# Merging the inverted 32-blocks of two heads in one pass in the gated DeltaNet layer

## The chip, the cores and the metric

The kernel runs on one core of one Trainium2 chip. The metric is the device time of one execution in microseconds (us). The time before is the median of three runs.

## The reference

The reference is a two-layer encoder trunk over 1040 positions (16 meta tokens and 1024 inputs, width 1024). Layer A is a gated DeltaNet with 8 heads of 128; layer B is multi-head latent attention that reads keys and values built after layer A. The change lies in layer A. Per chunk the reference solves a unit lower triangular system for u and w and then scans a state over the chunks:

```python
    decay = jnp.exp(jnp.where(tril, gc[..., :, None] - gc[..., None, :], -jnp.inf))
    kb = k * beta[..., None]
    lower = jnp.where(tril_strict, jnp.einsum('bhnid,bhnjd->bhnij', kb, k) * decay, 0.0)
    system = lower + jnp.eye(c, dtype=jnp.float32)
    rhs = jnp.concatenate([v * beta[..., None], kb * jnp.exp(gc)[..., None]], -1)
    sol = lax.linalg.triangular_solve(system, rhs, left_side=True, lower=True)
    u_base, w_dec = sol[..., :dv], sol[..., dv:]
...
    def step(state, xs):
        u0, wd, qd, att, kd, gl = xs
        u = u0 - jnp.einsum('bhck,bhkv->bhcv', wd, state)
        o = jnp.einsum('bhck,bhkv->bhcv', qd, state) + jnp.einsum('bhij,bhjv->bhiv', att, u)
        state = state * gl[..., None, None] + jnp.einsum('bhck,bhcv->bhkv', kd, u)
        return state, o
```

## The kernel before

Layer A works on 8 token tiles of 128 and the 16 meta tokens as a tile of their own, and takes chunks of 128 instead of 64, which is the same computation. The inputs to a head (key, value and query columns) each come from a GEMM in split precision (`mm3`, lines 91 to 93, three matmuls for each of eight 128-row steps, in three chunks of 272, 384 and 384 tokens), a causal convolution with SiLU (`conv_acts`: copy on ScalarE L370, first tap on GpSimd L372, three taps on VectorE L375). The weight columns are loaded on SyncE's queue (L203) and split on GpSimd or VectorE (L98, L99).

Heads are taken in pairs. For a pair, in program order: `prepare` calls `key_prep` for each head. It builds the decay matrices `att` and the strictly triangular products `U`, one 128x128 block for each token tile, and stores the 32x32 blocks on the diagonal of `U` to DRAM (`blk_in`, L462), together with the meta block `Um`. `invert_blocks` then inverts all 66 blocks of the pair at once (32 blocks and one meta block for each head, one block per partition) in 31 steps on VectorE (L525, L528), clears one triangle on GpSimd (L530) and stores the result to `blk_out` (L532).

`finish_inverse(h, N)` merges four inverted 32-blocks into one 128x128 inverse, for one head and its eight token tiles. `N` is the tile `U` itself, overwritten in place. The tile `T64` (one buffer) gets the four inverted 32-blocks of each token tile by four loads from `blk_out` (L545); VectorE transposes each into `N` (L546), 32x256 a time. The meta block takes the same way through `Xm` (one buffer, L547) and `Nm` (L548). There are then four stages, each with eight tiles of matmuls into the single bank `fin`, and an eviction of it:

1. L555, two 32x32 products a tile; VectorE multiplies by -beta into `T64` (L557, twice).
2. L560 and L562, three 32x32 products a tile; ScalarE copies them to `T64` and `N` (L563, and L565 twice).
3. L568, one 64x64 product a tile; VectorE multiplies by -beta (L569).
4. L572, one 64x64 product a tile; ScalarE copies to `N` (L573).

A float32 matmul is two instructions in the trace. The result `N` is read by the scan (`scan_tile`, L600), and `Nm` by `scan_meta` (L579). The scans of the two heads alternate by token tile and share the bank tag `ch`; a scan step goes from PE to VectorE and back several times (L595, L597, L599, L600, L602, L605, L607, L609).

The program is written in the order of the main loop (below), but each engine's order of issue is set when the kernel is built: instructions whose inputs are expected to be ready can be issued ahead of earlier ones that are expected to wait, by program order otherwise. So GEMM matmuls of the next heads stand between the stages of the merge and the steps of the scan on PE, and parts of the next pair's `key_prep` start before the scan has ended. Each engine then runs its own queue strictly in that order; semaphores make an instruction wait, and all behind it on that engine.

Of the kernel before, what the change touches and what calls it, by code (L numbers as in the profile page):

```python
# [16 lines left out]
F32 = mybir.dt.float32  # L17
# [3 lines left out]
ALU = mybir.AluOpType  # L21
PSUM = bass.MemoryType.PSUM

P = 128
D = 1024
NM = 16
T = 1024
L = NM + T
NT = T // P
# [87 lines left out]
def body(ctx: ExitStack, tc: tile.TileContext, I, out):  # L117
    nc = tc.nc
    V, A, G, TE, SY = nc.vector, nc.scalar, nc.gpsimd, nc.tensor, nc.sync
    tpool, nm, act, mm3, split_w, split_ps = tools(tc)  # L120
# [11 lines left out]
    blk_out = [dram(f"blk_out{i}", [66, 32, 32]) for i in range(2)]  # L132
# [49 lines left out]
    with ExitStack() as la:  # L182
# [5 lines left out]
        def bank(tag, shape):  # L188
            return pp.tile(shape, F32, tag=tag, name=nm(tag), bufs={'mm': 2, 'tr': 3, 'fin': 1, 'ch': 2}[tag])
# [25 lines left out]
        with ExitStack() as l0:  # L215
# [9 lines left out]
            n = 0  # L225
# [15 lines left out]
            for c, (a, b) in enumerate(TOKC):  # L241
                tiles = [t for t in range(-1, NT) if a <= tok(t)[0] < b]
# [12 lines left out]
                for kt in range(KT):  # L255
                    ps = bank("tr", [P, 512])
# [4 lines left out]
        with ExitStack() as l0:  # L261
# [8 lines left out]
            for c, (a, b) in enumerate(TOKC):  # L270
                ps = bank("fin", [P, 512])[0:4 * H, 0:b - a]
                for kt in range(KT):
                    w = wab2[:, kt].rearrange("p x c -> p (x c)")
# [5 lines left out]
            ps = bank("tr", [P, 512])  # L279
            for t in range(-1, NT):  # L280
                a, b = tok(t)
# [13 lines left out]
            def ntile(name, w=NT + 1):  # L295
# [4 lines left out]
            beta, g, egc, ekd, necb, egl, epsq, nbeta = (ntile(x) for x in (  # L300
                "beta", "g", "egc", "ekd", "necb", "egl", "epsq", "nbeta"))
# [20 lines left out]
            ps = bank("tr", [P, 512])  # L322
# [17 lines left out]
        kp = ld.enter_context(tpool(name="kA", bufs=2))  # L340
        sp = ld.enter_context(tpool(name="sA", bufs=2))
        bp = ld.enter_context(tpool(name="bA", bufs=1))
# [37 lines left out]
        def halves():  # L380
            return [(hf, slice(4 * hf, 4 * hf + 4)) for hf in range(2)]

        def key_prep(h, kn):

            att, kd = ([kp.tile([P, 4, P], F32, tag=y, name=nm(y), bufs=6) for _ in range(2)] for y in ("att", "kd"))
            U = kp.tile([P, NT, P], F32, tag="U", name=nm("U"), bufs=4)
            kdm = sp.tile([NM, P], F32, tag="kdm", name=nm("kdm"), bufs=3)
            hc = slice(h, h + 1)
            flat = lambda x: x.rearrange("p a b -> p (a b)")
# [2 lines left out]
            for half, s4 in halves() + [(2, slice(NT, NT + 1))]:  # L392
                k, tiles = (P, range(s4.start, s4.stop)) if half < 2 else (NM, (-1,))
                ps = bank("tr", [P, 4, P])
                junk = sp.tile([P, P], BF16, tag="jk", name=nm("junk"), bufs=1)
                for j, t in enumerate(tiles):
                    a, b = tok(t)
# [5 lines left out]
                if half < 2:  # L403
                    V.tensor_tensor(out=kd[half], in0=ps, in1=sc4[:, :, None].broadcast_to([P, 4, P]),
                                    op=ALU.mult)
                else:
                    V.tensor_scalar(out=kdm, in0=ps[0:k, 0, :], scalar1=sc4, scalar2=None, op0=ALU.mult)
            for rows, s in ((slice(0, P), slice(0, NT)), (slice(0, NM), slice(NT, NT + 1))):
                x = lambda y: flat(y[rows, s, hc])
# [4 lines left out]
            ps = bank("tr", [P, 512])  # L414
# [9 lines left out]
            for half, s4 in halves():  # L424
                ps = bank("tr", [P, 512])
                for i in range(2):
                    s2 = slice(s4.start + 2 * i, s4.start + 2 * i + 2)
                    gs = [bp.tile([P, 2, P], F32R, tag=f"g{y}", name=nm("gm")) for y in range(2)]
                    for y, gy in enumerate((ghi, glo)):
# [5 lines left out]
                                op=ALU.mult)  # L435
                G.affine_select(out=att[half], in_=att[half], compare_op=ALU.is_ge, fill=0.0, base=0,
                                pattern=[[0, 4], [1, P]], channel_multiplier=-1)
                ps = bank("tr", [P, 512])
                for j in range(4):
                    a, b = tok(4 * half + j)  # L440
                    TE.matmul(ps[:, P * j:P * j + P], kn[:, a:b], kn[:, a:b], start=True, stop=True)
                V.tensor_tensor(out=U[:, s4, :], in0=ps.rearrange("p (t i) -> p t i", i=P),
                                in1=att[half], op=ALU.mult)
            attm = sp.tile([NM, NM], F32, tag="attm", name=nm("attm"), bufs=3)
# [4 lines left out]
            ps = bank("tr", [P, 512])  # L449
# [11 lines left out]
                r = slice(32 * q, 32 * q + 32)  # L461
                SY.dma_start(dst[q], U[r, :, r])  # L462
            SY.dma_start(blk_in[gi][33 * hl + 32, 0:NM, 0:NM], Um)
            return dict(att=att, attm=attm, U=U, kd=kd, kdm=kdm)

        def query_prep(h, c):

            qT, kn, att, attm = c["qT"], c["kn"], c["att"], c["attm"]
            sq = kp.tile([P, L], F32, tag="vT", name=nm("sq"), bufs=1)
            ps = bank("tr", [P, 512])  # L470
            for a, b in TOKC:
                act(sq[:, a:b], qT[:, a:b], AF.Square)
            for t in range(-1, NT):
                a, b = tok(t)
                s = t if t >= 0 else NT
                TE.matmul(ps[0:b - a, s:s + 1], sq[:, a:b], one, start=True, stop=True)
            for rows, s in ((slice(0, P), slice(0, NT)), (slice(0, NM), slice(NT, NT + 1))):
                V.tensor_scalar(out=epsq[rows, s, h:h + 1].rearrange("p t o -> p (t o)"), in0=ps[rows, s],
                                scalar1=EPS * P, scalar2=EPS * EPS * P, op0=ALU.mult, op1=ALU.add)
            for half, s4 in halves():  # L480
                ps = bank("tr", [P, 512])
                for j in range(4):
                    a, b = tok(4 * half + j)
                    TE.matmul(ps[:, P * j:P * j + P], kn[:, a:b], qT[:, a:b], start=True, stop=True)  # L484
                V.tensor_tensor(out=att[half], in0=ps.rearrange("p (t i) -> p t i", i=P),
                                in1=att[half], op=ALU.mult)
            ps = bank("tr", [P, 512])
            TE.matmul(ps[:NM, 0:NM], kn[:, 0:NM], qT[:, 0:NM], start=True, stop=True)
            V.tensor_tensor(out=attm, in0=ps[:NM, 0:NM], in1=attm, op=ALU.mult)
# [41 lines left out]
                            channel_multiplier=0)  # L531
            SY.dma_start(blk_out[gi].rearrange("p a b -> p (a b)"), flat)  # L532

        def finish_inverse(h, N):

            gi, hl = (h // 2) % 2, h % 2
            Nm = sp.tile([32, 32], F32, tag="Nm", name=nm("Nm"), bufs=3)
            Xm = bp.tile([32, 32], F32, tag="Xm", name=nm("Xm"))
            T64 = bp.tile([P, NT, 64], F32, tag="T64", name=nm("T64"))
            q0, q1, q2, q3 = qs = [slice(32 * q, 32 * q + 32) for q in range(4)]  # L540
            lo32, hi32 = slice(0, 32), slice(32, 64)
            G.memset(T64[q0, :, hi32], 0.0)
            blk = blk_out[gi][33 * hl:33 * hl + 32].rearrange("(t q) i j -> q i t j", q=4)
            for q, c in ((0, lo32), (1, hi32), (2, lo32), (3, hi32)):
                SY.dma_start(T64[qs[q], :, c], blk[q])  # L545
                V.transpose(N[qs[q], :, qs[q]], T64[qs[q], :, c])  # L546
            SY.dma_start(Xm, blk_out[gi][33 * hl + 32])  # L547
            V.transpose(Nm, Xm)  # L548
            bt = lambda rows, w: nbeta[rows, 0:NT, h:h + 1].broadcast_to([rows.stop - rows.start, NT, w])
            ps = bank("fin", [P, NT, 64])  # L550
            Z = T64[:, :, lo32]
            lo64, hi64 = slice(0, 64), slice(64, P)
            for t in range(NT):
                for a, b in ((q0, q1), (q2, q3)):
                    TE.matmul(ps[b, t, 0:32], N[a, t, b], T64[a, t, 0:32], start=True, stop=True)  # L555
            for b in (q1, q3):
                V.tensor_tensor(out=Z[b], in0=ps[b, :, 0:32], in1=bt(b, 32), op=ALU.mult)  # L557
            ps = bank("fin", [P, NT, 64])
            for t in range(NT):
                TE.matmul(ps[q1, t, 0:32], N[q1, t, q1], Z[q1, t, :], start=True, stop=True)  # L560
                for a, b in ((q0, q1), (q2, q3)):
                    TE.matmul(ps[a, t, 32:64], Z[b, t, :], N[b, t, b], start=True, stop=True)  # L562
            A.copy(T64[q1, :, 0:32], ps[q1, :, 0:32])  # L563
            for a, b in ((q0, q1), (q2, q3)):
                A.copy(N[a, :, b], ps[a, :, 32:64])  # L565
            ps = bank("fin", [P, NT, 64])
            for t in range(NT):
                TE.matmul(ps[hi64, t, :], N[lo64, t, hi64], T64[lo64, t, :], start=True, stop=True)  # L568
            V.tensor_tensor(out=T64[hi64], in0=ps[hi64], in1=bt(hi64, 64), op=ALU.mult)  # L569
            ps = bank("fin", [P, NT, 64])  # L570
            for t in range(NT):
                TE.matmul(ps[lo64, t, :], T64[hi64, t, :], N[hi64, t, hi64], start=True, stop=True)  # L572
            A.copy(N[lo64, :, hi64], ps[lo64])  # L573
            return dict(N=N, Nm=Nm[0:NM, 0:NM])

        def scan_meta(h, c):
            ps = bank("ch", [P, 512])
# [42 lines left out]
        def keys_of(h):  # L620
            hs[h]["kn"] = conv_acts(D + h * P, "kn", 4)
# [8 lines left out]
            hs[h]["vb"], hs[h]["vbm"] = natural(hs[h]["vT"], beta, h, "vb")  # L630

        def prepare(h0):
            for h in (h0, h0 + 1):
                hs[h].update(key_prep(h, hs[h]["kn"]))
            invert_blocks((h0 // 2) % 2, h0)

        def finish(h):
            hs[h].update(finish_inverse(h, hs[h]["U"]))

        keys_of(0)  # L640
        keys_of(1)
# [1 line left out]
        for h0 in range(0, H, 2):  # L643
            h1, more = h0 + 1, h0 + 2 < H
            values_of(h0)
            value_rows(h0)
            values_of(h1)
            queries_of(h0)
            value_rows(h1)
            queries_of(h1)  # L650
            query_prep(h0, hs[h0])
            finish(h0)
            if more:
                keys_of(h0 + 2)
            query_prep(h1, hs[h1])
            if more:
                keys_of(h1 + 2)
            finish(h1)
            Ss = {h: scan_meta(h, hs[h]) for h in (h0, h1)}
            for t in range(NT):  # L660
                for h in (h0, h1):
                    Ss[h] = scan_tile(h, t, hs[h], Ss[h])
            if more:
                prepare(h0 + 2)
# [791 lines left out]
```

## Time and profile before

| | |
|---|---|
| median of 3 runs | 1362.63 us |
| lowest, highest | 1353.95 us, 1364.2 us |
| the profiled execution | 1358.79 us, span 1357.1 us |
| granted TensorE clock in it, mean | 0.989 |
| busy: PE, VectorE, ScalarE, GpSimd | 1313.5, 905.6, 537.2, 408.7 us |

The profile is of one execution. PE is TensorE's matmuls, PEld its weight loads, DVE VectorE, ACT ScalarE, POOL GpSimd, SP (SPq) SyncE, which issues the DMAs. L555 is line 555 of the kernel. In a group of instructions `fin<-T,U` names what is written and what is read (`T` is `T64`, buffer numbers are left out); then come the shapes, the count after an x, and the least, median and longest duration in ns. In the order of time the columns are start and duration in us, and in brackets the idle time ahead of the instruction and what ended it; a row with x16 stands for sixteen instructions in a row, from the start of the first to the end of the last. In the list of waits the columns are the total in us, how many, and the longest. Layer A takes the first half of the span, up to about 640 us.

### The profile page before, as it was taken

How to read it: one execution, taken by the hardware profiler on the slowest of the kernel's cores; microseconds unless marked ns; L12 is line 12 of the kernel's file. 1: busy time of each engine (PE TensorE's matmuls, PEld its weight loads, DVE VectorE, ACT ScalarE, POOL GpSimd, SP SyncE). 2: the span in 40 equal slices, each digit the busy share in tenths (PEclk: the TensorE clock that was granted, in tenths of full speed). 3: DMA queues.
4: the chain of work that ended last, by engine and by line, in shares of the span. 5: the costliest groups of instructions: out<-in, count | busy, mean ns of one | idle time of the engine just before them, and what ended most of it. 6: DMA issues, size and time to landing. Idle time of an engine off the chain costs nothing.

```text
span 1357.1 us, 24958 instructions
## 1 busy us (share of the span) xinstructions
PE 1313.5 (97%) x9064; PEld 1184.5 (87%) x9064; DVE 905.6 (67%) x2625; ACT 537.2 (40%) x1706; POOL 408.7 (30%) x684
## 2 busy tenths in 40 slices
PE   6999999999999999999999999998999999999998
PEld 4879989988998999898788798887999999998887
DVE  6679768968996895545464665323887879778321
ACT  6442243233324331211132243115777777776200
POOL 3344223423342130042010401321544445337100
PEclk9999989999999999999999999999999999999999
DMA  6111112121111213126552202312111101014443
GB/s 186 39 27 46 46 24 52 48 49 31 50 47 36 47 47 91 54 82 206 173 167 87 83 13 64 109 66 69 36 42 32 54 24 41 17 36 136 136 149 111
DMA packets 116924, 96.81 MB, mean 71 GB/s; under 512 B 28462, under 2 KB 106094, under 8 KB 116802
## 3 DMA queue, kind: packets, MB, share of 16 engines
q1 hardware_dynamic: 116802, 95.23, 23.3%
q8 instruction: 71, 1.16, 0.4%
q14 instruction: 51, 0.42, 0.1%
HBM read 68.19 MB, written 27.01 MB: 70 GB/s over the span
## 4 chain that ended last, share of the span: by engine, by line
PE 76%; DVE 8%; POOL 6%; ACT 4%; DMA 3%; issue 2%; SPq 0%; DVEq 0%; POOLq 0%; ACTq 0%
PE mm L93 7%; PE mm L91 7%; PE mm L92 7%; PE sc L93 6%; PE sc L92 6%; PE sc L91 6%; PE bd L91 4%; PE bd L92 4%; PE bd L93 4%; PE pt L1298 2%; PE tr L484 1%; PE ch L599 1%; PE ch L595 1%; ACT junk L82 1%; PE ch L609 1%
## 5 line engine op out<-in xcount | busy, mean ns | idle before, releaser
L91 PE MATMUL mm<-hT_hi,whi 128*128 128x384 f32 (+1 forms) x768 | 257.0, 335 | 2.4 <-DVE whi L98 2.4
L93 PE MATMUL mm<-hT_hi,wlo 128*128 128x384 f32 (+1 forms) x768 | 256.0, 333 | 0.5 <-DVE wlo L99 0.5
L92 PE MATMUL mm<-hT_lo,whi 128*128 128x384 f32 (+1 forms) x768 | 255.4, 333 | 0.0
L91 PEld LDWEIGHTS mm<-hT_hi,whi 128*128 128x128 f32 x768 | 146.8, 191 | 4.0 <-issue 2.9
L93 PEld LDWEIGHTS mm<-hT_hi,wlo 128*128 128x128 f32 x768 | 146.9, 191 | 3.3 <-DVE wlo L99 1.1
L92 PEld LDWEIGHTS mm<-hT_lo,whi 128*128 128x128 f32 x768 | 147.2, 192 | 1.3 <-issue 0.8
L108 DVE TENSOR_TENSOR pTl<-pt,pTh 128x256 fp32r<-128x256 f32 (+2 forms) x112 | 55.0, 494 | 11.0 <-ACT pTh L107 9.6
L98 POOL TENSOR_SCALAR whi<-raw 128x512 fp32r<-128x512 f32 x48 | 38.5, 816 | 73.2 <-PE mm L92 67.1
L82 ACT ACTIVATE P<-P,mx 128x144 f32<-128x144 f32 (+3 forms) x64 | 50.6, 791 | 21.3 <-DVE mx L1256 18.7
L91 PE MATMUL sc<-wo_hi,oTh 128*128 128x512 f32 (+1 forms) x144 | 57.6, 400 | 0.6 <-issue 0.6
L93 PE MATMUL sc<-wo_hi,oTl 128*128 128x512 f32 (+1 forms) x144 | 57.2, 397 | 0.0
L92 PE MATMUL sc<-wo_lo,oTh 128*128 128x512 f32 (+1 forms) x144 | 57.0, 396 | 0.0
L370 ACT COPY z<-mm 128x384 f32<-128x384 f32 (+1 forms) x72 | 31.8, 442 | 62.1 <-PE mm L93 61.6
L99 DVE TENSOR_TENSOR wlo<-raw,whi 128x512 fp32r<-128x512 f32 x64 | 47.3, 745 | 10.6 <-POOL whi L98 10.4
L375 DVE SCALAR_TENSOR_TENSOR kn<-z,pcol,kn 128x384 f32<-128x384 f32 (+1 forms) x72 | 42.3, 589 | 17.4 <-POOL kn L372 16.5
L107 ACT CAST pTh<-pt 128x256 fp32r<-128x256 f32 (+2 forms) x112 | 47.2, 427 | 14.6 <-PE pt L1298 7.2
L1269 POOL TENSOR_SCALAR P<-P,sl 128x144 f32<-128x144 f32 (+3 forms) x64 | 51.5, 806 | 3.7
L1267 POOL TENSOR_SCALAR Pe<-P,sl 128x128 f32<-128x128 f32 x64 | 29.5, 462 | 73.3 <-DVE sl L1264 55.6
L93 PE MATMUL sc<-h_hi,wlo 128*128 128x512 f32 x128 | 50.8, 397 | 0.0
L92 PE MATMUL sc<-h_lo,whi 128*128 128x512 f32 x128 | 50.6, 396 | 0.0
L91 PE MATMUL sc<-h_hi,whi 128*128 128x512 f32 x128 | 50.5, 395 | 0.0
L102 DVE SCALAR_TENSOR_TENSOR wlo<-raw,pcol,whi 128x128 fp32r<-128x128 f32 x64 | 23.4, 429 | 40.3 <-POOL whi L101 40.3
(380 smaller groups left out, 3985.4 us busy)
## 6 DMA issues: line engine op xcount, KB each, us to landing
raw<-in_a_w_in SPq DMA_DIRECT2D x64, 256.0 KB
xt<-in_x SPq DMA_DIRECT2D x16, 512.0 KB
o_scr<-o SPq DMA_DIRECT2D x64, 64.0 KB
raw<-in_a_w_out SPq DMA_DIRECT2D x8, 512.0 KB
on<-o_scr SPq DMA_DIRECT2D x8, 512.0 KB
x_scr<-xt SPq DMA_DIRECT2D x8, 512.0 KB
raw<-in_b_w_in SPq DMA_DIRECT2D x8, 512.0 KB
gb_scr<-z SPq DMA_DIRECT2D x8, 512.0 KB
```

The source lines that it names most:

```text
L82: i = A.activation(out_ap, in_ap, func, **kw)
L91: TE.matmul(ps, ahi, bhi, start=first, stop=False)
L92: TE.matmul(ps, ahi, blo, start=False, stop=False)
L93: TE.matmul(ps, alo, bhi, start=False, stop=last)
L98: eng.tensor_scalar(out=hi, in0=raw, scalar1=1.0, scalar2=1.0, op0=ALU.mult, op1=ALU.mult)
L99: V.tensor_tensor(out=lo, in0=raw, in1=hi, op=ALU.subtract)
L107: A.copy(hi, ps)
L108: V.tensor_tensor(out=lo, in0=ps, in1=hi, op=ALU.subtract)
L370: A.copy(z[:, 3 + a:3 + b], gemm_T(hi, lo, c))
L375: V.scalar_tensor_tensor(out=yc, in0=z[:, a + j:b + j], scalar=col("cw", 24 * j + m), in1=yc, op0=ALU.mult, op1=ALU.add)
L1267: G.tensor_scalar(out=Pe, in0=Pm[:, None, 0:NM].broadcast_to([P, E8, NM]), scalar1=s, scalar2=1.0, op0=ALU.mult, op1=ALU.mult)
L1269: G.tensor_scalar(out=Pm[:, 0:n], in0=Pm[:, 0:n], scalar1=s, scalar2=1.0, op0=ALU.mult, op1=ALU.mult)
```

## The change

The two heads of a pair are merged in one pass. `U` becomes one tile `[P, 2, NT, P]` for a pair (2 buffers instead of 4 of half the size), and `T64` becomes `[P, 2, NT, 64]` (still one buffer). `finish_inverses(h0, N)` does what `finish_inverse` did for both heads: it loads the eight block groups first (quadrants in the order 0, 2, 1, 3, both heads of each), then takes the two meta blocks through `Xm` and `Nm`, then transposes each quadrant for both heads by one instruction of 32x512. Stages 1 and 2 put each head's products beside the other's in the bank `fin`, packed to 32 columns. In stages 3 and 4 the heads use different halves of the partitions of the bank (`to`): in stage 3 head 0 the upper half and head 1 the lower, in stage 4 the other way round. Evictions of stages 1 and 2 are done for both heads by one instruction, those of stages 3 and 4 head by head. In each stage the tiles of head 1 come first, then those of head 0.

In the main loop the one call stands behind the first of the next pair's keys and ahead of the second head's query preparation; before, the first head's call stood ahead of those keys, and the second head's behind the second of the next pair's keys, directly ahead of the scan.

```diff
-        def finish_inverse(h, N):
+        def finish_inverses(h0, N):
...
-            T64 = bp.tile([P, NT, 64], F32, tag="T64", name=nm("T64"))
+            T64 = bp.tile([P, 2, NT, 64], F32, tag="T64", name=nm("T64"))
...
-            G.memset(T64[q0, :, hi32], 0.0)
-            blk = blk_out[gi][33 * hl:33 * hl + 32].rearrange("(t q) i j -> q i t j", q=4)
-            for q, c in ((0, lo32), (1, hi32), (2, lo32), (3, hi32)):
-                SY.dma_start(T64[qs[q], :, c], blk[q])
-                V.transpose(N[qs[q], :, qs[q]], T64[qs[q], :, c])
-            SY.dma_start(Xm, blk_out[gi][33 * hl + 32])
-            V.transpose(Nm, Xm)
+            G.memset(T64[q0, :, :, hi32], 0.0)
+            cs = (lo32, hi32, lo32, hi32)
+            for q in (0, 2, 1, 3):
+                for hl in range(2):
+                    blk = blk_out[gi][33 * hl:33 * hl + 32].rearrange("(t q) i j -> q i t j", q=4)
+                    SY.dma_start(T64[qs[q], hl, :, cs[q]], blk[q])
+            for hl in range(2):
+                Nm = sp.tile([32, 32], F32, tag="Nm", name=nm("Nm"), bufs=3)
+                Xm = bp.tile([32, 32], F32, tag="Xm", name=nm("Xm"))
+                SY.dma_start(Xm, blk_out[gi][33 * hl + 32])
+                V.transpose(Nm, Xm)
+                Nms.append(Nm[0:NM, 0:NM])
+            tiles = lambda x: x.rearrange("p h t i -> p (h t) i")
+            for q, c in enumerate(cs):
+                V.transpose(tiles(N[qs[q], :, :, qs[q]]), tiles(T64[qs[q], :, :, c]))
...
+            each = [(hl, t) for hl in (1, 0) for t in range(NT)]
+            Z = T64[:, :, :, lo32]
+            ps = bank("fin", [P, 2, NT, 32])
+            for hl, t in each:
+                for a, b in ((q2, q3), (q0, q1)):
+                    TE.matmul(ps[b, hl, t], N[a, hl, t, b], T64[a, hl, t, 0:32], start=True, stop=True)
+            for b in (q1, q3):
+                V.tensor_tensor(out=Z[b], in0=ps[b], in1=bt(b, 0, 2, 32), op=ALU.mult)
+            ps = bank("fin", [P, 2, NT, 32])
+            for hl, t in each:
+                TE.matmul(ps[q1, hl, t], N[q1, hl, t, q1], Z[q1, hl, t], start=True, stop=True)
+                for a, b in ((q0, q1), (q2, q3)):
+                    TE.matmul(ps[a, hl, t], Z[b, hl, t], N[b, hl, t, b], start=True, stop=True)
+            A.copy(T64[q1, :, :, 0:32], ps[q1])
+            for a, b in ((q0, q1), (q2, q3)):
+                A.copy(N[a, :, :, b], ps[a])
+
             ps = bank("fin", [P, NT, 64])
+            to = ((hi64, lo64), (lo64, hi64))
+            for hl, t in each:
+                TE.matmul(ps[to[hl][0], t], N[lo64, hl, t, hi64], T64[lo64, hl, t], start=True, stop=True)
+            for hl in range(2):
+                V.tensor_tensor(out=T64[hi64, hl], in0=ps[to[hl][0]], in1=bt(hi64, hl, 1, 64)[:, 0], op=ALU.mult)
             ps = bank("fin", [P, NT, 64])
+            for hl, t in each:
+                TE.matmul(ps[to[hl][1], t], T64[hi64, hl, t], N[hi64, hl, t, hi64], start=True, stop=True)
+            for hl in range(2):
+                A.copy(N[lo64, hl, :, hi64], ps[to[hl][1]])
+            for hl in range(2):
+                hs[h0 + hl].update(N=N[:, hl], Nm=Nms[hl])
...
         def prepare(h0):
+            U = kp.tile([P, 2, NT, P], F32, tag="U", name=nm("U"), bufs=2)
             for h in (h0, h0 + 1):
-                hs[h].update(key_prep(h, hs[h]["kn"]))
+                hs[h].update(key_prep(h, hs[h]["kn"], U[:, h - h0]))
...
             query_prep(h0, hs[h0])
-            finish(h0)
             if more:
                 keys_of(h0 + 2)
+            finish_inverses(h0, hs[h0]["Us"])
             query_prep(h1, hs[h1])
             if more:
                 keys_of(h1 + 2)
-            finish(h1)
             Ss = {h: scan_meta(h, hs[h]) for h in (h0, h1)}
```

More of the change, by code (lines that the diff above doesn't have):

```diff
@@ L381, in halves, with key_prep @@
             return [(hf, slice(4 * hf, 4 * hf + 4)) for hf in range(2)]
-        def key_prep(h, kn):
+        def key_prep(h, kn, U):
             att, kd = ([kp.tile([P, 4, P], F32, tag=y, name=nm(y), bufs=6) for _ in range(2)] for y in ("att", "kd"))
-            U = kp.tile([P, NT, P], F32, tag="U", name=nm("U"), bufs=4)
             kdm = sp.tile([NM, P], F32, tag="kdm", name=nm("kdm"), bufs=3)
@@ L463, in key_prep @@
             SY.dma_start(blk_in[gi][33 * hl + 32, 0:NM, 0:NM], Um)
-            return dict(att=att, attm=attm, U=U, kd=kd, kdm=kdm)
+            return dict(att=att, attm=attm, kd=kd, kdm=kdm)
         def query_prep(h, c):
@@ L532, in invert_blocks @@
             SY.dma_start(blk_out[gi].rearrange("p a b -> p (a b)"), flat)
-        def finish_inverse(h, N):
-            gi, hl = (h // 2) % 2, h % 2
-            Nm = sp.tile([32, 32], F32, tag="Nm", name=nm("Nm"), bufs=3)
-            Xm = bp.tile([32, 32], F32, tag="Xm", name=nm("Xm"))
-            T64 = bp.tile([P, NT, 64], F32, tag="T64", name=nm("T64"))
+        def finish_inverses(h0, N):
+            gi = (h0 // 2) % 2
+            Nms = []
+            T64 = bp.tile([P, 2, NT, 64], F32, tag="T64", name=nm("T64"))
@@ L548, in finish_inverse @@
-            V.transpose(Nm, Xm)
-            bt = lambda rows, w: nbeta[rows, 0:NT, h:h + 1].broadcast_to([rows.stop - rows.start, NT, w])
-            ps = bank("fin", [P, NT, 64])
[L551 to L557, printed above, removed]
@@ L558, in finish_inverse @@
-            ps = bank("fin", [P, NT, 64])
[L559 to L574, printed above, removed]
+            G.memset(T64[q0, :, :, hi32], 0.0)
@@ new lines, in finish_inverses, with bt @@
+            tiles = lambda x: x.rearrange("p h t i -> p (h t) i")
+            for q, c in enumerate(cs):
+                V.transpose(tiles(N[qs[q], :, :, qs[q]]), tiles(T64[qs[q], :, :, c]))
+            def bt(rows, hl, n, w):
+                y = nbeta[rows, 0:NT, h0 + hl:h0 + hl + n].rearrange("p t h -> p h t")
+                return y[:, :, :, None].broadcast_to([rows.stop - rows.start, n, NT, w])
+            each = [(hl, t) for hl in (1, 0) for t in range(NT)]
+            Z = T64[:, :, :, lo32]
@@ new lines, in finish_inverses @@
+            lo64, hi64 = slice(0, 64), slice(64, P)
+            ps = bank("fin", [P, 2, NT, 32])
[9 more added lines that the diff above has]
+                    TE.matmul(ps[a, hl, t], Z[b, hl, t], N[b, hl, t, b], start=True, stop=True)
@@ L632, in prepare @@
         def prepare(h0):
+            U = kp.tile([P, 2, NT, P], F32, tag="U", name=nm("U"), bufs=2)
             for h in (h0, h0 + 1):
-                hs[h].update(key_prep(h, hs[h]["kn"]))
+                hs[h].update(key_prep(h, hs[h]["kn"], U[:, h - h0]))
+            hs[h0]["Us"] = U
             invert_blocks((h0 // 2) % 2, h0)
-        def finish(h):
-            hs[h].update(finish_inverse(h, hs[h]["U"]))
         keys_of(0)
```

## The prediction

> **What bounds the kernel now.** I read the page first, for the engine that sets the end and the one profiled execution's span.
>
> ```profile
> span 1357.1 us, 24958 instructions
> PE 1313.5 (97%) x9064; PEld 1184.5 (87%) x9064; DVE 905.6 (67%) x2625; ACT 537.2 (40%) x1706; POOL 408.7 (30%) x684
> PE   6999999999999999999999999998999999999998
> PE 76%; DVE 8%; POOL 6%; ACT 4%; DMA 3%; issue 2%; SPq 0%; DVEq 0%; POOLq 0%; ACTq 0%
> ```
>
> TensorE (PE) is busy 97% of the span, nine tenths or more in all but three of the forty slices, and makes up 76% of the chain that ended last. So the change is worth what it saves or costs in PE's own queue. The next view is the busy time by stretch, where I put the bounds round the places at which the inverse is merged and the scan runs (161 to 210 us for the first pair of heads, then 290 to 335, 415 to 460, 540 to 590), with one stretch of plain GEMM work (460 to 540) to compare.
>
> ```profile
> core 0: us, PE busy (x) PEld busy (x) DVE busy (x) ACT busy (x) POOL busy (x), PEclk, DMA share, GB/s
> 161.00:210.00 49.00, 47.47 (x467) 40.40 (x466) 35.48 (x123) 21.25 (x89) 12.62 (x26) 0.90 0.12 27
> 290.00:335.00 45.00, 44.05 (x472) 37.95 (x473) 34.46 (x119) 20.04 (x88) 11.96 (x23) 1.00 0.15 36
> 415.00:460.00 45.00, 44.57 (x472) 37.49 (x471) 35.16 (x127) 19.63 (x82) 10.41 (x23) 1.00 0.13 30
> 460.00:540.00 80.00, 79.70 (x614) 76.05 (x613) 63.42 (x177) 21.20 (x59) 14.95 (x18) 1.00 0.25 68
> 540.00:590.00 50.00, 50.00 (x443) 44.78 (x441) 29.51 (x94) 12.11 (x47) 1.95 (x2) 1.00 0.19 59
> ```
>
> Even where the merges and the scan run, PE is idle for only 1.53 + 0.95 + 0.43 + 0.00 = 2.91 us in all: the projection GEMMs of the next heads fill the waits. VectorE (DVE) has 10 to 20 us free in each of these four stretches. A shorter chain of merges is therefore worth little in itself; what counts is how much PE time the merges use.
>
> **The change part by part: PE.** The query on the tile of the merge bank (fin) gives every instruction of the merges.
>
> ```profile
> L555 PE MATMUL fin<-T,U x256: 190/191/258, 161.9 to 548.9; 32*32 32x32 f32 x128
> L562 PE MATMUL fin<-U,T x256: 190/191/213, 166.7 to 551.2; 32*32 32x32 f32 x128
> L560 PE MATMUL fin<-T,U x128: 185/191/213, 166.7 to 551.1; 32*32 32x32 f32 x128
> L568 PE MATMUL fin<-T,U x128: 218/218/268, 171.3 to 553.5; 64*64 64x64 f32 x128
> L572 PE MATMUL fin<-U,T x128: 217/218/366, 174.5 to 555.7; 64*64 64x64 f32 x128
> L557 DVE TENSOR_TENSOR T<-fin,nbeta x16: 417/424/431, 165.2 to 550.0; 32x256 f32<-32x256 f32 x16
> L565 ACT COPY U<-fin x16: 361/362/365, 169.5 to 552.1; 32x256 f32<-32x256 f32 x16
> L569 DVE TENSOR_TENSOR T<-fin,nbeta x8: 694/694/695, 172.5 to 553.8; 64x512 f32<-64x512 f32 x8
> L573 ACT COPY U<-fin x8: 578/579/582, 176.5 to 555.9; 64x512 f32<-64x512 f32 x8
> ```
>
> The matmuls stay: the new loops run over two heads and eight tiles, so the five rows keep 256, 256, 128, 128 and 128 instructions, with the same 32 by 32 and 64 by 64 shapes. What goes is visits. Between two stages of a head PE does other work, and each time it goes to the small shapes and comes back. Order of time on PE shows what that costs:
>
> ```profile
> 311.73 0.33 PE L92 MATMUL mm<-hT_lo,whi 128*128 128x384 f32 x1
> 311.90 0.34 PE L93 MATMUL mm<-hT_hi,wlo 128*128 128x384 f32 x1
> 312.16 1.14 PE L572 MATMUL fin<-U,T 64*64 64x64 f32 x16
> 313.24 0.28 PE L417 MATMUL tr<-ident,br 128*8 128x128 f32 x1
> ...
> 184.22 0.69 PE L555 MATMUL fin<-T,U 32*32 32x32 f32 x30
> 184.84 0.17 PE L418 MATMUL tr<-ident,br 16*1 16x16 f32 x1
> ```
>
> One GEMM matmul follows the last by 0.17 us (311.73 to 311.90), but the first L572 follows by 0.26: 0.09 us to get in. Sixteen L572 take 1.14 us to the end of the last, which itself lasts 0.218: fifteen steps of 0.92 / 15 = 0.061. From the first to the next foreign instruction are 1.08 us, so the last step is 1.08 - 0.92 = 0.16, or 0.10 to get out. For L555, thirty in 0.69 with 0.191 for the last make steps of 0.017; 0.62 to the next instruction leaves 0.12, again 0.10 to get out. A visit costs 0.09 + 0.10 = 0.19 us beside its matmuls.
>
> [...]
>
> How many visits? Four stages a head, and the first comes in two pieces, as the chain shows:
>
> ```profile
> 181.87 0.24 PE fin L555 x2
> 184.29 0.62 PE fin L555 x30
> ```
>
> So 5 visits for each of 8 heads, 40 in all; with a pair in one pass, 5 for each of 4 pairs, 20. **20 x 0.19 = 3.8 us saved.** The bounds: nothing, if the order of issue cuts the longer stages up again, and 20 x 0.26 = 5.2 if the first matmul's whole step of 0.26 went.
>
> **DVE and ScalarE (ACT).** From 32x256 to 64x512 a DVE eviction grows from 424 to 694 ns, 1.05 ns a column and about 154 ns for the instruction; an ACT copy grows from 362 to 579, about 145 ns for the instruction. A pair loses 2 multiplies and 3 copies: 0.31 us of DVE and 0.43 of ACT. The block transposes fall from 8 to 4; no 32x512 transpose is in the trace, so a merged one lies between one and two of the present ones:
>
> ```profile
> L546 DVE STREAM_TRANSPOSE U<-T x32: 425/435/442, 162.4 to 549.5; 32x256 f32<-32x256 f32 x32
> ```
>
> 0.44 to 0.87 us; I take 0.71, by the slope of the evictions, which saves 4 x 0.16 = 0.6 us a pair. All of it lies beside PE work, since DVE has 10 us and more free in each stretch: 0 in the sum, at most the 4 x 0.9 = 3.6 us of DVE if the GEMMs that cover it were gone.
>
> **GpSimd (POOL).** The memset of T64 waits for the tile's one buffer, until the head before has ended its last stage, and POOL's queue stands behind it:
>
> ```profile
> POOL T L542 <- PE fin L572: 30.2, 4, 16.3
> ...
> 176.57 0.30 POOL L542 MEMSET T<- 32x256 f32 x1 [8.25 <-PE fin L572]
> 180.99 0.41 POOL L430 TENSOR_SCALAR_AFFINE_SELECT gm<-ghi 128x256 fp32r<-128x256 f32 x1 [4.12 <-PE tr L432]
> ```
>
> With one tile for both heads this wait goes. But what is late next is PE: POOL's next instruction after the memset waits 4.12 us for a PE matmul, so POOL was not what PE missed. I take 0, with -1 us as the far end (a third of the 2.91 idle).
>
> **SyncE and the meta block.** Ten loads a pair stay ten, but the eight block loads now stand ahead of both Xm loads, and the two Xm transposes ahead of all block transposes. Xm has one buffer, so the second load waits for the first transpose:
>
> ```profile
> 159.17 1.82 SPq L545 DMA_DIRECT2D T<-blk_out  x4
> 161.03 0.45 SPq L547 DMA_DIRECT2D Xm<-blk_out  x1
> 166.77 0.31 SPq L547 DMA_DIRECT2D Xm<-blk_out  x1
> 170.38 0.20 DVE L548 STREAM_TRANSPOSE Nm<-Xm 32x32 f32<-32x32 f32 x1 [0.49 <-DMA Xm<-blk_out]
> ...
> PE ch L579 <- DVE Nm L548: 1.6, 2, 1.3
> ```
>
> An Xm load took 170.38 - 166.77 = 3.6 us from issue to use. That turn exists now, and PE waits 1.6 us in all for it at the meta scan (L579). In the new order the block transposes can stand behind two such turns in DVE's queue; behind those stand the conv steps of the next keys (L375), for which ACT and then the next key preparation wait. Stage 1 needs no transpose, so PE can start it; stage 2 is what would be late. Costs between -1.6 (the L579 wait goes) and 4 x 7.2 = 28.8 (both turns bare in four pairs); I take 0, nearest to the row of 1.6 in all, because GEMMs are ready for PE there. Weight loads queue behind the second Xm load on SyncE as they do now. [...]
>
> **Order.** Moving the pass behind the next pair's first keys costs nothing, as the block loads can't start before the inversion ends: in the first pair they are issued at 159.17, and L555 begins 2.7 us later, at 161.9. The second head's merge comes earlier, before its query preparation; its scan can begin with the other's. PE has the same work to do, so 0 in the sum, at most the 2.91 us of idle.
>
> **Sum.** -3.8 us. The profiled execution took 1358.79 us (span 1357.1 and 1.7 around it), so one like it would take 1355.0. The median of the three runs shown, 1362.63, lies 3.8 us higher; on that footing the forecast is 1358.8.
>
> **The rivals.**
> - *Cut up again.* The change doesn't do what it says: other work is issued between the halves of the merged stages, as between the 2 and the 30 of L555. Visits stay near 40, time 1362.6. For: that cut exists in the chain now; against: the 16 and 30 matmul runs above are otherwise unbroken.
> - *Everything falls into place.* The 3.8 us, the 2.91 us of idle and the 1 to 2 us of slower steps around them go: -8, 1354.6. To pass 1% it would need 13.6 us, which no row shows in these stretches.
> - *The Xm turns are bare* (slower). DVE stands at the second Xm transpose, the block transposes wait, PE reaches stage 2 with its order fixed and waits. With one turn bare in each pair 4 x 3.6 - 3.8 = +10.6, 1373.2; with both 4 x 7.2 - 3.8 = +25.0, 1387.6. It passes 1% from (13.6 + 3.8) / 4 = 4.4 us of bare wait a pair. For: PE does wait for Nm at L579. Against: DVE has stood for a block load before, 6.25 us up to 531.51, and PE was idle 0.30 us in the whole stretch from 460 to 540:
>
> ```profile
> 531.51 1.42 DVE L546 STREAM_TRANSPOSE U<-T 32x256 f32<-32x256 f32 x3 [6.25 <-DMA T<-blk_out]
> ```
>
> **How the numbers follow.** Forecast 0.56, cut up again 0.18, everything in place 0.13, bare turns 0.13. A change of 1% (13.6 us) is about what a measurement of this kernel can tell from none: the runs shown lie between 1353.95 and 1364.2. Faster by over 1%: half of the good case and a little for an order that I don't see, 0.10. Slower by over 1%: half of the bare turns and as much for order, 0.10. Within 1%: 0.80. The range goes from 1349 (the good case, and half the 10.2 us spread of the runs shown below it) to 1375 (one turn bare in each pair, and 2 us of spread): it leaves out about 0.10 on each side.
>
> **What would show it.** Right: the five matmul rows keep their counts, and runs of 32 and about 60 stand in PE's order of time where 16 and 30 stood; the multiplies of stage 1 are 8 of 32x512 at about 0.69 us, the copies 12 at about 0.58, the transposes 16; POOL's wait of 30.2 us is gone and the span hardly shorter for it; PE idle in the four stretches stays under 3 us. Wrong: a long wait of DVE for Xm ahead of the block transposes with PE idle at stage 2, runs still of 16 and 30, steps inside a run other than 0.061 and 0.017, or a change of many us in stretches without merges, which would mean that the order of all the rest has moved.

## The result and the profile after

The changed kernel takes 1351.3 us in the median of 14 runs (1347.6 to 1355.0), the kernel before, on the same chip, 1361.5. The ratio is 0.9938 (95% interval 0.9921 to 0.9955), or 8.4 us less. A second comparison, of 12 runs, gave 1352.1 and a ratio of 0.9950 (0.9925 to 0.9975). The forecast was 1358.8, 3.8 us less than the 1362.6 of the three runs before: right in sign and inside its range, with under half of the gain. Both profiled executions ran at the same mean clock, 0.989, so the pages can be set side by side. First the page of the changed kernel:

```profile
span 1350.1 us, 24895 instructions
PE 1306.3 (97%) x9064; PEld 1181.7 (88%) x9064; DVE 900.1 (67%) x2601; ACT 534.8 (40%) x1694; POOL 412.8 (31%) x680
```

The span is 7.0 us shorter and PE's busy time 7.2. PE executes 9064 matmuls as before, so nearly all of the gain is that the same matmuls take less of PE's time; a drop in PE's idle time is not where it lies. The busy time by stretch, with the bounds of before:

```profile
161.00:210.00 49.00, 48.50 (x524) 42.76 (x523) 40.14 (x141) 23.82 (x94) 14.79 (x31) 1.00 0.13 31
290.00:335.00 45.00, 44.49 (x358) 40.03 (x357) 37.67 (x136) 18.46 (x77) 14.56 (x30) 1.00 0.11 24
415.00:460.00 45.00, 44.69 (x360) 41.16 (x358) 36.01 (x126) 17.27 (x69) 11.69 (x25) 1.00 0.14 32
460.00:540.00 80.00, 79.15 (x697) 75.23 (x696) 56.91 (x149) 18.71 (x49) 18.42 (x14) 0.98 0.24 64
540.00:590.00 50.00, 50.00 (x343) 47.21 (x342) 26.59 (x83) 10.00 (x40) 15.16 (x10) 1.00 0.27 80
```

PE's idle in the four stretches falls from 2.91 to 1.32 us, but rises from 0.30 to 0.85 between 460 and 540, into which the last pair's merges (up to 535) now fall. The granted clock, the number behind POOL's, is 1.00 in the first stretch, where it was 0.90.

The merge bank's instructions, by tile, and the order of time on PE in the first pair:

```profile
L566 PE MATMUL fin<-T,U x256: 190/191/212, 163.5 to 522.2; 32*32 32x32 f32 x128
L573 PE MATMUL fin<-U,T x256: 191/191/212, 167.6 to 527.2; 32*32 32x32 f32 x128
L571 PE MATMUL fin<-T,U x128: 191/191/212, 167.5 to 527.2; 32*32 32x32 f32 x128
L581 PE MATMUL fin<-T,U x128: 218/218/267, 172.2 to 530.9; 64*64 64x64 f32 x128
L586 PE MATMUL fin<-U,T x128: 218/218/267, 176.5 to 535.3; 64*64 64x64 f32 x128
L568 DVE TENSOR_TENSOR T<-fin,nbeta x8: 683/690/698, 165.4 to 523.2; 32x512 f32<-32x512 f32 x8
L576 ACT COPY U<-fin x8: 574/576/577, 170.3 to 528.6; 32x512 f32<-32x512 f32 x8
L574 ACT COPY T<-fin x4: 576/577/577, 169.7 to 527.5; 32x512 f32<-32x512 f32 x4
```

```profile
163.46 1.20 PE L566 MATMUL fin<-T,U 32*32 32x32 f32 x64
164.59 0.33 PE L397 MATMUL tr<-ident,kn 128*128 128x128 f32 x1
...
172.15 1.90 PE L581 MATMUL fin<-T,U 64*64 64x64 f32 x32
173.98 0.71 PE L597 MATMUL ch<-um,kdm 16*128 16x128 f32 x4
```

All five counts and durations are kept. Stage 1 is one run of 64, stages 3 and 4 are runs of 32. Only stage 2 is cut: 4 of its 96 instructions come 0.9 us ahead of the rest here, up to 1.9 us in the other pairs. By the records there are 20 visits where there were 40; counted as runs with nothing between, 23 and 42, since in three of the new runs and two of the old a single 16x16 matmul of the meta scan (L595; L579 in the kernel before) stands in the middle.

### The profile page after: what moved, and what is told of

The parts are those of the page before. It is cut to its first block, busy times and chain, and to the rows that moved or that the text cites. A ratio compares the mean times of both kernels' runs of the same rounds, so it can differ in the third digit from the quotient of the medians.

```text
span 1350.1 us, 24895 instructions
## 1 busy us (share of the span) xinstructions
PE 1306.3 (97%) x9064; PEld 1181.7 (88%) x9064; DVE 900.1 (67%) x2601; ACT 534.8 (40%) x1694; POOL 412.8 (31%) x680
## 4 chain that ended last, share of the span: by engine, by line
PE 75%; DVE 8%; DMA 5%; POOL 5%; ACT 4%; issue 3%; SPq 0%; DVEq 0%; ACTq 0%; POOLq 0%
PE mm L91 7%; PE mm L93 7%; PE mm L92 7%; PE sc L93 6%; PE sc L92 6%; PE sc L91 6%; PE bd L91 3%; PE bd L93 3%; PE bd L92 3%; PE pt L1312 2%; PE tr L483 1%; DMA raw<-in_a_w_out 1%; ACT junk L82 1%; DMA out<-raw 1%; PE ch L625 1%
## 5 line engine op out<-in xcount | busy, mean ns | idle before, releaser
L91 PE MATMUL bd<-wf_hi,oTh 128*128 128x512 f32 x128 | 50.2, 392 | 0.3 <-ACT oTh L1422 0.2
```

The source lines that it names most:

```text
L91: TE.matmul(ps, ahi, bhi, start=first, stop=False)
```

## The experiments

One more column of the results is needed to read them. Executions of one kernel differ by several us, and each time goes with its mean granted clock: fitted over the runs of each kernel with 12 or 14 runs, 0.001 of clock stands for 0.7 to 1.4 us. (As an estimate from the span: if half clock for D us loses D/2 of work, 0.001 of mean clock is 1.36 us where PE's clock sets the pace.)

| kernel | median us | ratio to before (95%) | mean clock |
|---|---|---|---|
| before | 1359.1 to 1361.5 | 1 | 0.987 |
| changed | 1351.3; 1352.1 | 0.9938; 0.9950 (intervals above) | 0.989 |
| x1: new place alone | 1360.0 | 1.0002 (0.9971 to 1.0032) | 0.987 |
| y1: changed, all stages head by head | 1359.9 | 1.0005 (0.9987 to 1.0023) | 0.982 |
| x2: changed, stages 3 and 4 head by head | 1365.5 | 1.0039 (1.0011 to 1.0068) | 0.978 |
| y4: before, two buffers for T64 | 1361.0 | 0.9994 (0.9962 to 1.0026) | 0.985 |
| y2: before, two buffers for Xm | 1358.1 | 0.9998 (0.9977 to 1.0019) | 0.986 |
| x4: before, both | 1361.8 | 0.9998 (0.9969 to 1.0026) | 0.983 |
| x3: changed, 64 small matmuls added | 1383.4 | 1.0177 (1.0137 to 1.0216) | 0.979 |
| x6: x2 with dense matmuls added | 1360.2 | 0.9999 (0.9979 to 1.0019) | 0.991 |
| x7: changed, norms spread out | 1356.1 | 0.9954 (0.9935 to 0.9973) | 0.990 |
| x5: changed, heads take turns | 1347.5 | 0.9894 (0.9871 to 0.9918) | 0.989 |
| y3: x5, two buffers for Xm | 1347.9 | 0.9914 (0.9889 to 0.9939) | 0.987 |

The changed kernel ran again beside the first of them:

> The changed kernel once more, to stand beside the others on one chip. Theory A (visits: PE pays about 0.2 us each time it goes to the small shapes and back, and 20 such visits go) gives -4 us of the 8 to 10 us measured and leaves the rest open. Theory B (order: the second head's merge and scan start earlier, whatever the number of visits) gives all 8 to 10. Both expect about 8 us below before here.

**The place alone (x1).** The kernel before, with both calls at the new place:

```diff
             query_prep(h0, hs[h0])
-            finish(h0)
             if more:
                 keys_of(h0 + 2)
+            finish(h0)
+            finish(h1)
             query_prep(h1, hs[h1])
...
-            finish(h1)
             Ss = {h: scan_meta(h, hs[h]) for h in (h0, h1)}
```

> The kernel before, its two separate merges called one after the other at the place of the changed kernel's one call; 40 visits stay. Theory A: within 2 us of before (no visit goes). Theory B: 8 us faster than before, like the changed kernel. If both have a part: about 4 us faster.

1360.0, ratio 1.0002: the place alone gives nothing, within the 4 us of the interval. The pass at the old place was not run.

**Sharing alone (y1, x2).** y1 keeps the place, the paired loads, the paired transposes and the pair's `T64`, and does the matmul stages head by head, each with its own bank. x2 does so for stages 3 and 4 only:

```diff
-            for hl, t in each:
-                TE.matmul(ps[to[hl][0], t], N[lo64, hl, t, hi64], T64[lo64, hl, t], start=True, stop=True)
+            for hl in (0, 1):
+                ps = bank("fin", [P, NT, 64])
+                for t in range(NT):
+                    TE.matmul(ps[hi64, t], N[lo64, hl, t, hi64], T64[lo64, hl, t], start=True, stop=True)
...
```

> The changed kernel with all four matmul stages of the merges done head by head again, each with its own bank: 40 visits to the small modes where the changed kernel has 20 to 23, while the paired block loads, the paired transposes, the pair's 64-tile (so no wait of POOL for it) and the place in the program stay. Theory of the visits (0.24 us each, counted in the trace of before): 17 to 20 visits more, 4 to 5 us slower than the changed kernel at the same granted clock, so 1356 to 1357 at 0.989; where the longer stretch of small matmuls also lowers the clock, as stages 3 and 4 alone by head did (0.978), 1362 to 1366. Theory of the waits (what the changed kernel gained at equal clock is the 30.2 us of POOL's waiting and the single buffers): equal to the changed kernel at the same clock, 1351 to 1352 at 0.989.

> The changed kernel with stages 3 and 4 head by head again (two more evictions of the bank in a row, 28 visits instead of 20). Theory A: 8 visits more, 8 x 0.2 = 1.6 us slower than the changed kernel, so about 6.5 us faster than before. Theory B: as the changed kernel. If the longer chain through the one bank counts: 4 us or more slower than the changed kernel.

y1 measured 1359.9: in the measured time all of the gain is gone, so sharing the stages is worth about 8 us, and the loads, the transposes and the single memset show nothing without it. But the theory of the visits alone gave 1356 to 1357, and the clock is lower too, 0.982 for 0.989. Runs at one clock, 0.985 to 0.986, divide it otherwise: 15 of the kernel before took 1362.3 us in the mean, three of y1 1355.9, two of the changed kernel 1353.9. They are few, but by them y1 keeps most of the gain at an equal clock, sharing is worth some 2 us there, and the rest of its 8 us is the clock. x2 is slower still at 0.978. Its trace, by stretch, shows the clock at one half in the merges' last stages, with PE busy all the time:

```profile
170.00:176.30 6.30, 5.87 (x54) 4.53 (x55) 4.57 (x20) 2.14 (x6) 0.76 (x2) 1.00 0.01 3
176.30:186.60 10.30, 10.30 (x61) 9.21 (x59) 3.30 (x8) 2.61 (x9) 1.94 (x5) 0.50 0.01 2
```

The kernel before has such a stretch too, and the changed one has none there (PE alone, before first, then changed):

```profile
172.80:183.00 10.20, 10.20 (x49) 0.50 0.09 14
```

```profile
172.80:183.00 10.20, 10.20 (x109) 1.00 0.01 2
```

In these 10.20 us the kernel before issues 49 matmuls and the changed one 109. They aren't the same matmuls, but the next lines of before show the price for one and the same group, stage 4 at half clock and at full (the first is from the first head's merge):

```profile
174.49 1.97 PE L572 MATMUL fin<-U,T 64*64 64x64 f32 x16
...
191.85 1.14 PE L572 MATMUL fin<-U,T 64*64 64x64 f32 x16
192.92 0.49 PE L599 MATMUL ch<-S,qT 128*128 128x128 f32 x2
193.25 0.39 PE L600 MATMUL ch<-r,U 128*128 128x128 f32 x2
193.47 0.38 PE L398 MATMUL tr<-ident,kn 128*128 128x128 f32 x2
```

To divide the gain I went through all PE steps between 100 and 600 us of four traces: each step from one start to the next, less the median step of that instruction outside half-clock stretches.

```
us between 100 and 600               before  changed    y1     y4
lost at half clock                     12.0      8.7   13.5   18.6
visits (in, out, the step after)       10.2      4.6    8.8    8.4
time inside the runs of merges         24.5     22.4   24.3   24.2
other steps late by over 0.1           14.5     15.8   14.9   10.1
```

From before to changed: -5.6 for the visits, -2.1 inside the runs, -3.3 at half clock, +1.3 for other late steps. Over the whole span the half-clock losses are equal (16.3 and 16.2 us), so the two profiles' 7.0 us are, by this count, the visits and the runs (7.7, less the 1.3). In the medians another 2 us or so are clock (0.987 to 0.989). For y1 the count divides the 8 us less sharply: visits and runs 6.1, half clock 7.9 over the span, which is 3.6 more than the 10.4 us between the two spans; and y1's clock alone, at 0.7 to 1.36 us for 0.001, makes 5 to 9. How much of sharing's 8 us is visits and how much clock stays open: 6.1 us of visits and runs by this count of y1's one profiled execution (1362.2 us, the third slowest of its twelve), some 2 us by the runs at one clock.

**The waits (y4, y2, x4).** Two buffers in the kernel before, for `T64`, for `Xm`, for both:

```diff
-            Xm = bp.tile([32, 32], F32, tag="Xm", name=nm("Xm"))
-            T64 = bp.tile([P, NT, 64], F32, tag="T64", name=nm("T64"))
+            Xm = bp.tile([32, 32], F32, tag="Xm", name=nm("Xm"), bufs=2)
+            T64 = bp.tile([P, NT, 64], F32, tag="T64", name=nm("T64"), bufs=2)
```

> The kernel before with two buffers instead of one for T64 and for Xm; nothing merged, 40 visits stay. The waits of GpSimd for T64 (30.2 us in the profile before) and of the second Xm load go. Theory A (visits and the clock): within 2 us of before. Theory C (the waits for the single buffers are what the merge took away): 6 to 8 us faster.

> The kernel before with two buffers for the 64-tile alone: POOL's wait of 30.2 us in all is gone and the second head's inverse can start while the first one's merges run. Theory of the waits with the 64-tile as their place: 1353 to 1354 at a clock of 0.989, but with the heads' merges close together the clock falls to about 0.983, so 1359 to 1362. If the wait is not on the path: 1358 at 0.989, and 1360 or slower measured.

> The kernel before with two buffers for the mask tile Xm alone, everything else as before. The kernel before with two buffers for both the 64-tile and Xm was 5 us faster at an equal clock and lost that to a clock of 0.983. If the gain sits in Xm: 1353 to 1356 at 0.989, with a clock like that of before, since the two heads' merges stay as far apart as they were. If it sits in the 64-tile: as before, 1358 at 0.989 (1360 measured).

All three are where the kernel before is. y4's list of waits shows that the wait didn't go, against what was expected, but fell from 30.2 us:

```profile
POOL T L542 <- PE fin L572: 18.9, 5, 7.0
```

In the count above y4 has 4.4 us less of other late steps than before and 6.6 more at half clock; a long stretch of it begins in its first pair's merges:

```profile
174.20:194.70 20.50, 20.50 (x178) 17.46 (x177) 9.08 (x38) 4.95 (x18) 3.64 (x9) 0.50 0.02 5
```

So by the count and the fit the waits are worth some 4 to 5 us (fitted to a clock of 0.989, x4 and y4 come to about 1353, before to 1358 to 1359), and in y4, whose merges follow each other sooner, as much is lost through the clock (6.6 us by the count). That makes the waits a rival of the visits for the gain at an equal clock: at 0.990 and 0.991 four runs of y4, with 36 visits in its trace, took 1350.1 to 1352.4, and seven of the changed kernel 1347.6 to 1352.7. Against them speaks only the count above, where the changed kernel's other late steps didn't fall (14.5 to 15.8). No run parts the two. Between y2 and before the difference is too small to place anything in Xm.

**The price of a visit (x3).** One constant 32x32 matmul into an unread part of the bank in each of 64 scan steps of the changed kernel; the result is overwritten:

```diff
             TE.matmul(ps[:, 2 * P:3 * P], c["qT"][:, a:b], S, start=True, stop=True)
+            TE.matmul(ps[0:32, P:P + 32], ident[0:32, 0:32], ones[0:32, 0:32], start=True, stop=True)
             TE.matmul(ps[:, P:2 * P], c["N"][:, t, :], r, start=True, stop=True)
```

> The changed kernel with one 32x32 matmul of constants more in each of the 64 scan steps, written where the next matmul of the step overwrites it. Theory A: 64 visits more, 64 x (0.19 + 2 x 0.02) = 13 to 15 us slower than the changed kernel, about 5 us slower than before. Without a price for a visit: 64 x 2 x 0.017 = 2 us slower than the changed kernel, 6 us faster than before.

31 us slower than the changed kernel, more than twice what any theory said. The clock fell from 0.989 to 0.979, which is 7 to 13 us; 18 to 25 remain, 0.28 to 0.39 us a visit. The order of time on PE shows one:

```profile
218.06 0.39 PE L615 MATMUL ch<-S,qT 128*128 128x128 f32 x2
218.38 0.24 PE L616 MATMUL ch<-ones,ident 32*32 32x32 f32 x2
218.55 0.49 PE L617 MATMUL ch<-r,U 128*128 128x128 f32 x2
218.88 0.49 PE L497 MATMUL tr<-ident,vT 128*128 128x128 f32 x3
```

A pair of 128x128 matmuls takes 0.22 us to the next start (193.25 to 193.47 above). Here the pair ahead of the visit takes 0.32, the two small instructions 0.17, and the pair behind it 0.33: 0.38 in all with the small ones, 0.21 without. The late step of the pair behind, 0.11, is what the prediction hadn't counted.

**The clock (x6, x7).** x6 is x2 with three matmuls of 128x384 from the projection's operands written into the bank ahead of each stage 3 and 4, where the stage overwrites them:

```diff
+                for _ in range(3):
+                    TE.matmul(ps.rearrange("p a b -> p (a b)")[:, 0:384], hT_hi[:, 0, 0:P], hT_hi[:, 1, 0:384],
+                              start=True, stop=True)
                 for t in range(NT):
                     TE.matmul(ps[hi64, t], N[lo64, hl, t, hi64], T64[lo64, hl, t], start=True, stop=True)
```

> The kernel with stages 3 and 4 head by head (1365.5 us at a mean granted clock of 0.978), with three dense 128x384 matmuls of no use ahead of the 16 matmuls of each stage 3 and 4: 8 x 2 x 3 x 0.174 = 8.4 us of PE work more. Theory D (a stretch of small matmuls in which few array cells work brings the clock to half for some us): the clock comes back to 0.988, worth 0.010 x 1160 = 12 us, so 1361 to 1363 us. Without such a link: clock 0.978, 1374 us.

48 matmuls more, and 5.2 us faster than x2. The stretch that stood at 0.50 in x2 stands at full clock:

```profile
176.30:186.60 10.30, 10.30 (x95) 8.88 (x94) 5.17 (x14) 3.60 (x13) 4.50 (x10) 1.00 0.04 10
```

With the wide matmuls between the small ones the clock stayed at 1.00 there, for 0.50 without. Idle time of PE doesn't part the two: PE is idle for 0.46 us between 170.0 and 176.3 in x6 and for 0.43 in x2, ahead of the halving, and x2's last merges are halved behind 10.20 us without any:

```profile
534.80:545.00 10.20, 10.20 (x173) 1.00 0.34 106
545.00:555.20 10.20, 10.20 (x56) 0.50 0.01 3
```

What it is in the small matmuls no run shows: their use of the array (Theory D), their number and their length aren't parted. In the kernel before, 1.34 us of idle do stand in the 6.80 us ahead of its stretch of 10.20; whether they had a part there is not shown.

Five of the changed kernel's half-clock stretches of 3.4 us begin 0.2 to 1.3 us behind the start of the last of the one-column matmuls of the query norms (L475, eighteen in a row, eight times in all; three times no such stretch follows), four of them without idle time in the 6.8 us ahead, as the first:

```profile
121.60:128.40 6.80, 6.80 (x47) 1.00 0.15 39
128.40:131.80 3.40, 3.40 (x17) 0.50 0.00 0
```

In x7 these were put between the 128-column products:

```diff
                     TE.matmul(ps[:, P * j:P * j + P], kn[:, a:b], qT[:, a:b], start=True, stop=True)
+                    TE.matmul(pn[:, t:t + 1], sq[:, a:b], one, start=True, stop=True)
```

> The changed kernel with the query norms' matmuls of one column (18 in a row now, after which the profile shows the clock at half for 3.4 us) each put between two of the 128-column products of the same step. Theory D: the dips after them go, up to 5 of 1.7 us each, clock 0.993, about 1346 us. Otherwise, or if the mixed stretch is as weak as before: 1352 us.

It missed: the clock rose by only 0.001, and it is 4 us slower than the changed kernel. Its profiled execution, the slowest of its twelve (1362.2 us), lies at 0.50 right after the first pair's merges, where the changed kernel's doesn't:

```profile
178.30:188.60 10.30, 10.30 (x66) 9.17 (x65) 3.84 (x10) 2.87 (x9) 3.40 (x8) 0.50 0.01 2
```

Its list of PE's waits has a row that the changed kernel's lacks:

```profile
PE tr L486 <- DVE att L480: 6.1, 4, 2.4
```

The edit holds the norms' bank (`pn`) through both halves of the products, so that with the two halves all three buffers of the tag `tr` are taken when the product of the meta tokens (L486) comes, and PE waits for VectorE to empty one. The changed kernel waits at that product 0.8 us in all. So x7 brought idle time by its own edit, in this execution more than the 4 us, and says little on the clock.

**Turns (x5, y3).** In stages 3 and 4 the heads write different halves of the bank's partitions. x5 lets them alternate tile by tile, and y3 adds a second `Xm`:

```diff
+            turns = [(hl, t) for t in range(NT) for hl in (1, 0)]
...
-            for hl, t in each:
+            for hl, t in turns:
                 TE.matmul(ps[to[hl][0], t], N[lo64, hl, t, hi64], T64[lo64, hl, t], start=True, stop=True)
```

> The changed kernel with the two heads in turns, tile by tile, in stages 3 and 4, so that neighbouring matmuls go to different halves of the array's columns. If the step of 0.061 us inside a run is set by neighbours that share a tile of the array, it falls towards 0.03: 256 x 0.03 = up to 7.7 us faster than the changed kernel (1344). If it is set by the rows, which the two heads share, it stays, and so does the time (1352).

> The changed kernel with the two heads taking turns tile by tile in the last two stages (1347.5 measured) and two buffers for Xm. If a wait for Xm costs anything there: up to 1.6 us less, 1346. If Xm comes in time anyway: 1347.5. If the earlier Xm puts the norms' one-column matmuls next to the merges, the clock falls and it is slower, 1350 to 1355.

```profile
171.59 1.15 PE L582 MATMUL fin<-T,U 64*64 64x64 f32 x32
172.67 0.71 PE L598 MATMUL ch<-um,kdm 16*128 16x128 f32 x4
...
175.21 1.15 PE L587 MATMUL fin<-U,T 64*64 64x64 f32 x32
```

The same 32 matmuls take 1.15 us for 1.90. The trace gives how much of the array each uses (64*64), not which rows and columns: that part of the expectation is not shown, the shorter step is. Eight such runs make 8 x 0.75 = 6.0 us, and the time fell by 4.6, to 1347.5: the best version of all. The second `Xm` adds nothing.

## Why the prediction was right, and where it was small

- *PE's time is what counts:* right. Span and PE busy time fell by 7.0 and 7.2 us.
- *40 visits become 20:* right by the records; "Cut up again" happened in stage 2 only, at 4 of 96 instructions (and at the single 16x16 matmuls). That the visits are where the gain at an equal clock comes from rests on the count of steps, not on a run.
- *0.19 us a visit:* this is the term that was too small. It took the entry (0.09) and the step of the last small matmul (0.10). The instruction after the first foreign one is late as well: L599 to L600 takes 0.33 us after stage 4 where 0.22 is usual. Over the trace of before the three parts are 0.10 + 0.09 + 0.05, 0.24 us for each of the 40 runs outside half-clock stretches, and in the changed one 0.18 for each of 23: 9.6 - 4.1 = 5.5 us instead of 3.8.
- *Steps inside a run stay 0.061 and 0.017:* stage 1 does, (1.20 - 0.191) / 63 = 0.016. Stage 3 goes to (1.90 - 0.218) / 31 = 0.054: the records show three matmuls of the one head starting beside one of the other at the seam (steps of 0.003 to 0.006). This, with the first step of a run, which takes 0.107 and is paid half as often, is most of the 2.1 us inside the runs; the prediction had 0.
- *The clock:* absent, though its own fence showed 0.90 for the first stretch. Some 2 us in the medians, and 0 between the two profiles. As a share of the measured gain this part was luck: nothing in the prediction foresaw it.
- *DVE and ACT off the path:* right; 690 and 576 ns for 0.69 and 0.58 predicted.
- *POOL's wait worth 0:* not shown. 30.2 us became 5.5 (below). y1, which has the pair's `T64` too and waits 12.2 us for it, is no faster than before in the median, but some 6 us faster at an equal clock, and y4 fits the same: the waits are worth something that the clock takes back there.

```profile
POOL T L540 <- PE fin L586: 5.5, 2, 4.0
```

- *The Xm turns bare:* didn't happen. In DVE's order of time the block transposes, L554, came before the two meta transposes, L550, though the program has these first (in the third pair one came between the two), so in no pair a block transpose stood behind the second `Xm` load:

```profile
167.30 0.70 DVE L554 STREAM_TRANSPOSE U<-T 32x512 f32<-32x512 f32 x1
168.03 0.20 DVE L550 STREAM_TRANSPOSE Nm<-Xm 32x32 f32<-32x32 f32 x1
168.68 0.50 DVE L375 SCALAR_TENSOR_TENSOR vT<-z,pcol,vT 128x272 f32<-128x272 f32 x1
170.38 0.48 DVE L375 SCALAR_TENSOR_TENSOR vT<-z,pcol,vT 128x272 f32<-128x272 f32 x1
170.87 0.19 DVE L550 STREAM_TRANSPOSE Nm<-Xm 32x32 f32<-32x32 f32 x1
```

- *Order worth 0:* right within the 4 us that x1 can tell.
- *Everything falls into place, -8:* the number came true, by other terms: it wanted 2.91 us from idle PE, and between 160 and 600 us PE is idle for 3.59 us before and 3.37 after (before first):

```profile
160.00:600.00 440.00, 436.41 (x3593) 0.98 0.19 51
```

```profile
160.00:600.00 440.00, 436.63 (x3652) 0.98 0.21 55
```

## What to carry to other kernels

Where PE sets the time, as here with 97% busy, count how often it changes between small tiles and full ones, and price a change by three steps: the first small one, the last small one, and the second full one after it (0.10, 0.09 and 0.05 us in the trace of before). Put independent small matmuls into one run, and try those that write different halves of a bank's partitions in turns (1.15 us for 1.90 in x5). Read the granted clock of each stretch with the waits: y4, where the merges follow each other sooner, had 4.4 us less of late steps and 6.6 more at half clock. Compare two kernels at the same granted clock before a difference is put down to a cause.

## What the runs showed of the hardware

The granted clock is 1.00 or 0.50 everywhere in the traces of before and of the changed kernel. Inside their spans it stands at 0.50 in stretches of 3.4 us (six before, nine in the changed kernel) and in one of 10.2 (before, from 172.80); in y4 it is 0.50 from 174.20 to 194.70. PE was busy without a gap ahead of some of them: for 10.20 us of 10.20 in x2 up to 545.00. With three wide matmuls ahead of each stage 3 and 4 the clock was 1.00 from 176.30 to 186.60 (x6), where x2 has 0.50. What sets it to 0.50 the runs do not show.

Matmuls of 64x64 that read the same partitions and write different halves of the bank's start closer together in turns: (1.15 - 0.218) / 31 = 0.030 us a step (x5) instead of (1.14 - 0.218) / 15 = 0.061 in a head's own run (before). In the kernel's time that went with 4.6 us, from 1352.1 to 1347.5.
